# An encoder layer in split float32: two sums of a weight quad in one addition, and a fourth seven-product quad in four of eleven gate-and-up groups

## The chip, the cores and the metric

The kernel runs on one core of a Trainium2 chip. The metric is device time in microseconds (us) for one execution of the whole layer; the median of several executions is compared. Engines are named as in the profile: PE is the matrix engine (TensorE), DVE the vector engine, ACT the scalar engine, POOL is GpSimd and SP the engine whose queue issues most DMAs.

## The reference, cut to what matters

The layer takes x of 256 rows by 2048 columns, mixes tokens with two kinds of attention, and ends in a SwiGLU feed-forward block. Only that block is touched:

```python
D_MODEL = 2048; SEQ = 256; D_FF = 5632
gt, up = jnp.split(rms_norm(x, g_ffn) @ w_gate_up, 2, axis=-1)   # w_gate_up: 2048 x 11264
return x + (jax.nn.silu(gt) * up) @ w_down                       # w_down: 5632 x 2048
```

All arrays are float32.

## The kernel before

**Split products.** PE takes float32r operands here. Each float32 matrix is split into a high part (a cast to float32r, on ACT) and a low part (the value less its high part, on DVE); `split_pair` does this for weights. `mm3` then computes one product as three matmuls of 128 x 128 by 128 x 512: high by high, high by low, low by high (lines 427 to 429). A weight chunk costs one cast and one subtraction over its whole width before PE can use it.

**Parts, groups, quads.** The feed-forward block runs in five parts. Part one covers three blocks of 512 hidden columns, parts two to five cover two each. A part first computes one *gate-and-up group* per block (11 groups in all), then four *down groups*, which multiply the hidden block by `w_down` and add to the residual. A gate-and-up group walks 2048 input rows in eight *quads*, numbered 0 to 7. A quad holds two row blocks of 128 (kk = 0, 1) of the gate columns and of the up columns (n = 0, 1), so four weight blocks of 128 x 512, one chunk `x` in SBUF of shape 128 x 4 x 512. The 256 tokens are two halves (t = 0, 1). The group wants the four sums over kk of h[t, kk] times w[kk, n].

**Plain and fast quads.** A plain quad does this with eight products, 24 matmuls. A *fast* quad uses Winograd's scheme for two-by-two blocks: seven products, 21 matmuls, on sums of blocks. Before, quads 2, 4 and 6 of every group are fast (`FAST`). For a fast quad `split_fast` splits three of the raw weight blocks (`rh`, `rl`: the two blocks of kk = 1; `r`: the up block of kk = 0), then makes four sums in place in `x` with four additions of 512 columns (lines 844 to 847); `split` then splits the four sums (`wh`, `wl`). The token side has the same two forms, made once by `job_h`: `hP` for plain quads, `hs`, `hsh`, `hsl` (seven blocks) for fast ones.

**PSUM.** During the block the eight 512-column banks are held as tiles `mA`, `mB`, `sC`, `sD`. Fast-only products go to `mA` and `mB`, the rest to `sC` and `sD`, which plain quads use too. After a group's last fast quad `evac_fast` reads `mA` and `mB` (lines 663 to 667). After its last quad `evac_pair` reads `sC` and `sD` (lines 677 to 680), then come the silu (ACT, line 683) and the product with the up half (line 685). The next quad that writes `sC` waits for lines 678 and 679. The down groups use `mA`, `mB`, `sC` and again `mA`; line 703 adds them to the residual tiles `x1_0` to `x1_3`.

**Order and buffers.** The instructions of the block are recorded in program order, and a scheduler with priorities then sets the order on each engine; every engine runs its own list in order. Weight chunks have three buffers `x` (`xp`), and three pairs `wh`, `wl` (six buffers, `wp`). The load of chunk c therefore starts when the low part `wl` of chunk c - 3 is done, and the cast `wh` of chunk c can start when PE has finished chunk c - 3. Loads are DMAs of 512 KB, two to a chunk, issued by SP (line 826 for quads, line 835 for the rest). Everything else (`rh`, `rl`, `r`, `z`, `u`, `hs`, hidden tiles) shares 28 buffers of one size (`tp`).

**Chunk numbers.** In the listings of order below, `x253` is the chunk of quad 0 of part two's first group, `x254` that of quad 1, up to `x260` for quad 7; `x261` to `x268` are the part's second group, and `x250` to `x252` the last chunks of part one's down groups. The first group of part one has chunks 217 to 224.

Of the kernel before, what the change touches and what calls it, by code (L numbers as in the profile page):

```python
# [12 lines left out]
F32 = mybir.dt.float32  # L13
# [27 lines left out]
PRIO = 200  # L41
NPAIR = KD // 2
FAST = (2, 4, 6)


class Job:
    def __init__(self, gen, after=()):
        self.gen, self.after, self.ready, self.done = gen, tuple(after), 0, False
# [16 lines left out]


class Group:
    def __init__(self, w, c0, n, ks, lhs, evac, needs=None, sizes=None):
        self.w, self.c0, self.n, self.ks = w, c0, n, ks
        self.lhs, self.evac, self.needs = lhs, evac, needs or {}  # L70
        self.sizes = sizes


class Quad:


    def __init__(self, group, i):
        self.group, self.i, self.fast = group, i, i in FAST
        plain = [k for k in range(NPAIR) if k not in FAST]
        self.first, self.last = i == plain[0], i == plain[-1]  # L80
        self.first_fast, self.last_fast = i == FAST[0], i == FAST[-1]


class Flag:
# [11 lines left out]
def layer_kernel(ctx: ExitStack, tc: tile.TileContext, a: dict, out: bass.AP):  # L96
# [12 lines left out]
    def t4(shape, name, dt=F32):  # L109
        return tp.tile(shape, dt, name=name, tag="t4")  # L110
# [108 lines left out]
    def split_pair(h, l, x):  # L219
        nc.scalar.copy(h, x)  # L220
        nc.vector.tensor_sub(l, x, f32(h))  # L221

    class Act:


        def __init__(self, name, nk):
            self.name, self.nk = name, nk
            self.h, self.l = {}, {}
# [384 lines left out]
    def job_h(i):  # L613

        ps = half_side(f"tr_h{i}").rearrange("p (k s) -> p k s", s=S)
        for k in range(2):
            f = 2 * i + k
            for t in range(NT):
                nc.tensor.transpose(ps[:, k, t * P:(t + 1) * P], x1[f // 4][:, t, (f % 4) * P:(f % 4 + 1) * P], ident)
        g = [gain("g_ffn", 2 * i + k) for k in range(2)]  # L620
        if i not in FAST:
            hP[i] = t4([P, 2, 2, S], f"hP{i}", F32R)
            split_evac(*((hP[i][:, 0, k], hP[i][:, 1, k], ps[:, k], g[k]) for k in range(2)))
        else:
            v, l, h = t4([P, 8, P], f"hs{i}"), t4([P, 7, P], f"hsl{i}", F32R), t4([P, 7, P], f"hsh{i}", F32R)
            nc.scalar.activation(v[:, 0:8:7], ps[:, 0].rearrange("p (t s) -> p t s", t=NT), AF.Copy, scale=g[0])
            nc.scalar.activation(v[:, 1:3], ps[:, 1].rearrange("p (t s) -> p t s", t=NT), AF.Copy, scale=g[1])
            nc.vector.tensor_sub(v[:, 3], v[:, 7], v[:, 2])
            nc.vector.tensor_sub(v[:, 4], v[:, 7], v[:, 0])
            nc.vector.tensor_sub(v[:, 5], v[:, 0], v[:, 3])  # L630
            nc.vector.tensor_sub(v[:, 6], v[:, 1], v[:, 5])
            split_pair(h, l, v[:, :7])
            hq[i] = (h, l)
        return
        yield
# [34 lines left out]
    def evac_pair(half, i, last):  # L670

        def evac(zu, step):
            q = held["q"]
            z, u = zu
            add, sub = nc.vector.tensor_add, nc.vector.tensor_sub
            with tc.high_priority(offset=PRIO):
                add(z[:, 1], q[0], z[:, 1])
                add(z[:, 0], q[3], z[:, 0])
                add(u[:, 0], q[2], u[:, 0])  # L679
# [75 lines left out]
    for half, (j0, j1) in enumerate(PARTS):  # L755
        js = range(j0, j1)
        hidT[half] = Act(f"hid{half}", 4 * len(js))
        for i, j in enumerate(js):
            needs = {k: (lambda k=k: [hjobs[k]]) for k in range(NPAIR)}
            needs[FAST[0]] = lambda: list(hjobs.values())  # L760
            if i:
                needs[FAST[0]] = lambda half=half, i=i: [djobs[half, i - 1]]
            groups.append(Group(W["w_gate_up"], 512 * j, 1024, range(NPAIR), None, evac_pair(half, i, i == len(js) - 1), needs))
# [56 lines left out]
    def load(c):  # L820
        g, gi, ks, q = chunks[c]
        t = xt[c] = xp.tile([P, 4, 512], F32, name=f"x{c}", tag="x")
        if q:
            for kk in range(2):
                src = g.w[(2 * q.i + kk) * P:(2 * q.i + kk + 1) * P].rearrange("p (n f) -> p n f", n=2)
                nc.sync.dma_start(t[:, 2 * kk:2 * kk + 2], src[:, :, g.c0:g.c0 + 512])
            return
        if gi == 0 and c:
            load_x(ks[0] * P, (ks[-1] + 1) * P)
            if ks[-1] == KD - 1:  # L830
                load_rows()
        for o in range(0, len(ks), 2):
            sub = ks[o:o + 2]
            src = g.w[sub[0] * P:(sub[-1] + 1) * P, g.c0:g.c0 + g.n]
            nc.sync.dma_start(t[:, o:o + len(sub), :g.n], src.rearrange("(k p) n -> p k n", p=P))

    def split_fast(c):

        x = xt[c]
        rh, rl, r = (t4([P, 2, 512], f"{n}{c}", F32R) for n in ("rh", "rl", "r"))  # L840
        split_pair(rh, rl, x[:, 2:4])
        split_pair(r[:, 0], r[:, 1], x[:, 1])
        add = nc.vector.tensor_add
        add(x[:, 1], x[:, 0], x[:, 1])
        add(x[:, 0], x[:, 0], x[:, 2])
        add(x[:, 2], x[:, 1], x[:, 2])
        add(x[:, 3], x[:, 2], x[:, 3])  # L847
        raws[c] = {1: (r[:, 0], r[:, 1]), 3: (rh[:, 0], rl[:, 0]), 2: (rh[:, 1], rl[:, 1])}

    def split(c):  # L850
        g, gi, ks, q = chunks[c]
        if q and q.fast and c not in raws:
            split_fast(c)
        t = xt.pop(c)
        h = w8(f"wh{c}")
        h, l = (h, w8(f"wl{c}")) if gi >= ffn_at else (h[:, :2], h[:, 2:])
        s = (slice(None), slice(0, 4 if q else len(ks)), slice(0, 512 if q else g.n))
        split_pair(h[s], l[s], t[s])
        if q and q.fast:
            parts[c] = raws.pop(c) | {m: (h[:, n], l[:, n]) for n, m in enumerate((7, 5, 6, 4))}  # L860
        else:
            parts[c] = (h, l)

# [3 lines left out]
        return [j for k in ks if k in g.needs for j in g.needs[k]()]  # L867

    FACTOR = {1: 0, 2: 1, 4: 2, 5: 3, 7: 4, 6: 5, 3: 6}
    PLAIN = {(0, 0): 3, (0, 1): 2, (1, 0): 0, (1, 1): 4}  # L870

    def products_quad(c):
        q = chunks[c][3]
        bank, w = held["q"], parts.pop(c)
        if not q.fast:
            h, l = w
            for t, n in ((1, 0), (0, 0), (0, 1), (1, 1)):
                m = PLAIN[t, n]
                for kk in range(2):
                    s = slice(t * P, (t + 1) * P)  # L880
                    mm3(bank[m], hP[q.i][:, 0, kk, s], hP[q.i][:, 1, kk, s], h[:, 2 * kk + n], l[:, 2 * kk + n],
                        q.first and kk == 0, q.last and kk == 1)
# [177 lines left out]
```

## Time and profile before

| what | us |
|---|---|
| median of 3 runs | 1356.53 |
| lowest and highest of them | 1354.4 and 1360.9 |
| the profiled execution | 1356.11 |
| its span, first to last instruction | 1354.3 |
| PE busy within the span | 1339.5 |
| DVE busy | 949.1 |
| ACT busy | 652.2 |

The feed-forward block fills roughly the second half of the span, from about 635 us on. In the timeline a matmul row shows its start and a modelled duration of 0.39 us; matmuls overlap in the pipeline, so the distance between two starts is what one of them costs. The times of rows are us from the start of the span.

### The profile page before, as it was taken

To read this page: it belongs to the slowest core of one execution; us is meant where nothing else is said; L and a number is where in the kernel's file an instruction comes from. 1 tells how busy PE (TensorE), PEld (TensorE's weight loads), DVE (VectorE), ACT (ScalarE), POOL (GpSimd) and SP (SyncE) were. 2 spreads that over 40 slices of the span, in tenths; PEclk is the share of its full clock that TensorE was granted. 3 is DMA by queue.
4 is the path that set the end of the run, shared out by engine and by line. 5 is a ranking of instruction groups with operands and counts; after the bars stand their busy time and mean duration, and the time that the engine had idled before them with its cause. 6 is when DMAs were issued, how large, how long until landed. Compare 5 with 4: busy or idle time off the path is not lost.

```text
span 1354.3 us, 16169 instructions
## 1 busy us (share of the span) xinstructions
PE 1339.5 (99%) x6243; PEld 1126.0 (83%) x6243; DVE 949.1 (70%) x949; ACT 652.2 (48%) x724; POOL 34.3 (3%) x41
## 2 busy tenths in 40 slices
PE   8999999999999999999999999999999999999998
PEld 6899999988888888888788888888878888888886
DVE  5566777677645655567789756886798579857973
ACT  6455555454444444455455434454445345534541
POOL 1011112000000000000000000000000000000000
PEclk9999999999999999999999999999999999999999
DMA  7555555656556766676546665565457654754662
GB/s 247 179 175 161 161 170 167 184 161 176 174 186 205 212 188 202 209 235 207 201 158 213 221 187 183 191 213 190 157 185 245 191 186 172 229 190 163 214 214 93
DMA packets 138205, 257.14 MB, mean 190 GB/s; under 512 B 9192, under 2 KB 28688, under 8 KB 138128
## 3 DMA queue, kind: packets, MB, share of 16 engines
q1 hardware_dynamic: 137760, 255.96, 58.9%
q8 instruction: 49, 0.80, 0.2%
q14 instruction: 28, 0.23, 0.1%
q10 hardware_dynamic: 144, 0.13, 0.0%
q0 software_dynamic: 224, 0.01, 0.0%
HBM read 253.97 MB, written 2.10 MB: 189 GB/s over the span
## 4 chain that ended last, share of the span: by engine, by line
PE 94%; DVE 2%; issue 1%; DMA 1%; ACT 1%; SPq 0%; DVEq 0%; ACTq 0%
PE g L429 14%; PE g L427 14%; PE g L428 13%; PE sC L427 6%; PE sC L429 6%; PE sC L428 6%; PE mA L427 4%; PE mA L429 4%; PE mA L428 4%; PE sD L429 4%; PE sD L427 4%; PE sD L428 4%; PE mB L428 3%; PE mB L429 3%; PE mB L427 3%
## 5 line engine op out<-in xcount | busy, mean ns | idle before, releaser
L220 ACT CAST wh<-x 128x1024 fp32r<-128x1024 f32 (+3 forms) x349 | 465.3, 1352 | 437.0 <-DVE x L847 127.7
L221 DVE TENSOR_TENSOR wl<-x,wh 128x2048 fp32r<-128x2048 f32 x132 | 300.8, 2289 | 134.5 <-ACT wh L220 132.7
L221 DVE TENSOR_TENSOR wh<-x,wh 128x1024 fp32r<-128x1024 f32 (+2 forms) x217 | 250.6, 1172 | 113.1 <-ACT wh L220 111.9
L427 PE MATMUL g<-wh,xTh 128*128 128x512 f32 (+1 forms) x544 | 210.6, 387 | 0.6 <-ACT xTh L212 0.6
L429 PE MATMUL g<-wh,xTl 128*128 128x512 f32 (+1 forms) x544 | 207.9, 382 | 0.6 <-DVE xTl L217 0.6
L428 PE MATMUL g<-wh,xTh 128*128 128x512 f32 (+1 forms) x544 | 207.9, 382 | 0.0
L429 PEld LDWEIGHTS g<-wh,xTl 128*128 128x128 f32 x544 | 102.8, 189 | 17.6 <-DVE xTl L217 1.4
L427 PEld LDWEIGHTS g<-wh,xTh 128*128 128x128 f32 x544 | 102.8, 189 | 15.9 <-ACT xTh L212 0.9
L428 PEld LDWEIGHTS g<-wh,xTh 128*128 128x128 f32 x544 | 102.9, 189 | 15.4 <-DVE wh L221 0.4
L427 PE MATMUL sC<-wh,hP 128*128 128x512 f32 x220 | 86.1, 391 | 1.6 <-DVE u L679 1.5
L429 PE MATMUL sC<-wh,hP 128*128 128x512 f32 x220 | 85.7, 390 | 0.0
L429 PE MATMUL sD<-wh,hP 128*128 128x512 f32 x220 | 85.7, 389 | 0.0
L428 PE MATMUL sC<-wl,hP 128*128 128x512 f32 x220 | 85.7, 389 | 0.0
L427 PE MATMUL sD<-wh,hP 128*128 128x512 f32 x220 | 85.7, 389 | 0.0
L428 PE MATMUL sD<-wl,hP 128*128 128x512 f32 x220 | 85.7, 389 | 0.0
L220 ACT CAST rh<-x 128x1024 fp32r<-128x1024 f32 x33 | 34.7, 1051 | 36.1 <-DMA x<-in_w_gate_up_dram 36.1
L427 PEld LDWEIGHTS sC<-wh,hP 128*128 128x128 f32 x220 | 41.3, 188 | 12.3 <-issue 4.0
L427 PE MATMUL g<-wh,mTh 128*128 128x512 f32 x128 | 50.5, 394 | 0.0
L429 PE MATMUL g<-wh,mTl 128*128 128x512 f32 x128 | 49.9, 390 | 0.0
L428 PE MATMUL g<-wh,mTh 128*128 128x512 f32 x128 | 49.9, 390 | 0.0
L427 PEld LDWEIGHTS sD<-wh,hP 128*128 128x128 f32 x220 | 41.3, 188 | 8.6
L428 PEld LDWEIGHTS sD<-wl,hP 128*128 128x128 f32 x220 | 41.3, 188 | 8.6
(675 smaller groups left out, 2390.7 us busy)
## 6 DMA issues: line engine op xcount, KB each, us to landing
x<-in_w_gate_up_dram SPq DMA_DIRECT2D x176, 512.0 KB, 4.7
x<-in_w_down_dram SPq DMA_DIRECT2D x88, 512.0 KB, 5.0
x<-in_w_in_dram SPq DMA_DIRECT2D x79, 512.0 KB, 4.2
x<-in_w_in_dram SPq DMA_DIRECT2D x56, 448.0 KB, 3.6
x<-in_w_o_dram SPq DMA_DIRECT2D x32, 512.0 KB, 4.4
x<-in_w_o_mla_dram SPq DMA_DIRECT2D x16, 512.0 KB, 4.9
x<-in_w_o_dil_dram SPq DMA_DIRECT2D x16, 512.0 KB, 4.6
x<-in_w_ukv_dram SPq DMA_DIRECT2D x8, 512.0 KB, 4.0
```

The source lines that it names most:

```text
L220: nc.scalar.copy(h, x)
L221: nc.vector.tensor_sub(l, x, f32(h))
L427: nc.tensor.matmul(ps, ah, bh, start=first, stop=False)
L428: nc.tensor.matmul(ps, ah, bl, start=False, stop=False)
L429: nc.tensor.matmul(ps, al, bh, start=False, stop=last)
```

## The change

Three things change.

1. In `split_fast` the order of the two kk = 0 blocks in the chunk is swapped: up in place 0, gate in place 1. Two of the four sums (gate plus up of kk = 0, and gate of kk = 0 plus gate of kk = 1) then share the operand in place 1 and lie side by side, and one addition over 1024 columns, with that operand broadcast, makes both. Three additions remain in place of four, in every fast quad.
2. For that swap, a fast quad's kk = 0 blocks are loaded by two DMAs of 256 KB, one each, and the kk = 1 blocks by one of 512 KB as before: three DMAs in place of two.
3. In the first gate-and-up group of parts two to five quads 1, 3, 4 and 6 are fast (`FAST_1`), in all other groups 2, 4 and 6 as before. So there are 37 fast quads in place of 33. Token blocks 1 and 3 are needed in both forms now, so `job_h` makes the eight-block form (`EITHER`) for them, and splits eight blocks, not seven, for all of the five quads in `EITHER`; plain quads 1, 2 and 3 pick their factors from it by `BLOCK`.

```diff
 FAST = (2, 4, 6)
+FAST_1 = (1, 3, 4, 6)
+EITHER = tuple(sorted(set(FAST) | set(FAST_1)))
...
 def job_h(i):
-        if i not in FAST:
+        if i not in EITHER:
             hP[i] = t4([P, 2, 2, S], f"hP{i}", F32R)
...
-            v, l, h = t4([P, 8, P], f"hs{i}"), t4([P, 7, P], f"hsl{i}", F32R), t4([P, 7, P], f"hsh{i}", F32R)
+            v, l, h = (t4([P, 8, P], f"{n}{i}", d) for n, d in (("hs", F32), ("hsl", F32R), ("hsh", F32R)))
...
-            split_pair(h, l, v[:, :7])
+            split_pair(h, l, v)
...
-            needs[FAST[0]] = lambda: list(hjobs.values())
+            fast = FAST_1 if half and not i else FAST
+            needs[2] = lambda: list(hjobs.values())
             if i:
-                needs[FAST[0]] = lambda half=half, i=i: [djobs[half, i - 1]]
+                needs[2] = lambda half=half, i=i: [djobs[half, i - 1]]
...
 def load(c):
         if q:
             for kk in range(2):
+                if q.fast and kk == 0:
+                    for n in range(2):
+                        src = g.w[2 * q.i * P:(2 * q.i + 1) * P, n * DFF + g.c0:n * DFF + g.c0 + 512]
+                        nc.sync.dma_start(t[:, 1 - n], src)
+                    continue
                 src = g.w[(2 * q.i + kk) * P:(2 * q.i + kk + 1) * P].rearrange("p (n f) -> p n f", n=2)
                 nc.sync.dma_start(t[:, 2 * kk:2 * kk + 2], src[:, :, g.c0:g.c0 + 512])
...
 def split_fast(c):
         split_pair(rh, rl, x[:, 2:4])
-        split_pair(r[:, 0], r[:, 1], x[:, 1])
+        split_pair(r[:, 0], r[:, 1], x[:, 0])
         add = nc.vector.tensor_add
-        add(x[:, 1], x[:, 0], x[:, 1])
-        add(x[:, 0], x[:, 0], x[:, 2])
-        add(x[:, 2], x[:, 1], x[:, 2])
+        add(x[:, :2], x[:, 1:2].to_broadcast([P, 2, 512]), x[:, 0:3:2])
+        add(x[:, 2], x[:, 0], x[:, 2])
         add(x[:, 3], x[:, 2], x[:, 3])
...
+    BLOCK = {(0, 0): 0, (0, 1): 7, (1, 0): 1, (1, 1): 2}
 def products_quad(c):
+            def factors(kk, t):
+                if q.i in EITHER:
+                    return (z[:, BLOCK[kk, t]] for z in hq[q.i])
+                return (hP[q.i][:, e, kk, t * P:(t + 1) * P] for e in range(2))
```

**What moves on DVE.** This is DVE's list in the first group of part two, from the low part of quad 2's chunk (`wl255`) to that of quad 4's (`wl257`). Before:

```order
L221 TENSOR_TENSOR wl255_6410<-x255_6338,wh255_6409 128x2048
L221 TENSOR_TENSOR rl257_6441<-x257_6413,rh257_6440 128x1024
L221 TENSOR_TENSOR r257_6442<-x257_6413,r257_6442 128x512
L221 TENSOR_TENSOR wl256_6452<-x256_6381,wh256_6451 128x2048
L844 TENSOR_TENSOR x257_6413<-x257_6413 128x512
L845 TENSOR_TENSOR x257_6413<-x257_6413 128x512
L846 TENSOR_TENSOR x257_6413<-x257_6413 128x512
L847 TENSOR_TENSOR x257_6413<-x257_6413 128x512
L221 TENSOR_TENSOR wl257_6483<-x257_6413,wh257_6482 128x2048
```

After (its lines lie a few numbers further down; 852 is the wide addition, 853 and 854 the two others):

```order
L223 TENSOR_TENSOR wl255_6433<-x255_6361,wh255_6432 128x2048
L852 TENSOR_TENSOR x256_6393<-x256_6393 128x1024
L223 TENSOR_TENSOR rl257_6465<-x257_6436,rh257_6464 128x1024
L853 TENSOR_TENSOR x256_6393<-x256_6393 128x512
L223 TENSOR_TENSOR r257_6466<-x257_6436,r257_6466 128x512
L854 TENSOR_TENSOR x256_6393<-x256_6393 128x512
L852 TENSOR_TENSOR x257_6436<-x257_6436 128x1024
L853 TENSOR_TENSOR x257_6436<-x257_6436 128x512
L854 TENSOR_TENSOR x257_6436<-x257_6436 128x512
L223 TENSOR_TENSOR wl256_6475<-x256_6393,wh256_6474 128x2048
L223 TENSOR_TENSOR wl257_6503<-x257_6436,wh257_6502 128x2048
```

Quads 3 and 4 are both fast now, so the sums of two quads stand between `wl255` and `wl256`, where one plain split and the raw splits of one fast quad stood.

**The end of the same group on DVE.** After the change, from the low part of the next group's first chunk to the reads of `sC`:

```order
L223 TENSOR_TENSOR wl261_6632<-x261_6576,wh261_6631 128x2048
L666 TENSOR_TENSOR z1536_6660<-mA_5128,u1536_6661 128x512
L667 TENSOR_TENSOR u1536_6661<-mB_5129,z1536_6660 128x512
L668 TENSOR_TENSOR z1536_6660<-mB_5129,u1536_6661 128x512
L669 TENSOR_TENSOR z1536_6660<-mB_5129,z1536_6660 128x512
L223 TENSOR_TENSOR wl262_6678<-x262_6604,wh262_6677 128x2048
L680 TENSOR_TENSOR z1536_6660<-sC_5130,z1536_6660 128x512
L681 TENSOR_TENSOR u1536_6661<-sC_5130,u1536_6661 128x512
```

Nothing moved here: before, the same eight rows stand in the same order (lines 664 to 667, 678 and 679), the low part `wl262` ahead of the two reads of `sC`.

**SP's queue at the same place.** Before:

```order
L826 DMA x255_6338<-in_w_gate_up_dram 128x2x512 x2
L826 DMA x256_6381<-in_w_gate_up_dram 128x2x512 x2
L826 DMA x257_6413<-in_w_gate_up_dram 128x2x512 x2
L826 DMA x258_6455<-in_w_gate_up_dram 128x2x512 x2
L826 DMA x259_6486<-in_w_gate_up_dram 128x2x512 x2
```

After (line 831 is the 256 KB load, 834 the 512 KB load):

```order
L834 DMA x255_6361<-in_w_gate_up_dram 128x2x512 x2
L831 DMA x256_6393<-in_w_gate_up_dram 128x512 x2
L834 DMA x256_6393<-in_w_gate_up_dram 128x2x512
L831 DMA x257_6436<-in_w_gate_up_dram 128x512 x2
L834 DMA x257_6436<-in_w_gate_up_dram 128x2x512
L834 DMA x258_6478<-in_w_gate_up_dram 128x2x512 x2
L831 DMA x259_6506<-in_w_gate_up_dram 128x512 x2
L834 DMA x259_6506<-in_w_gate_up_dram 128x2x512
```

The kk = 1 blocks, which the first cast of a fast quad (`rh`) reads, now come as the third DMA of the chunk, behind two small ones.

More of the change, by code (lines that the diff above doesn't have):

```diff
@@ L67, with __init__ @@
 class Group:
-    def __init__(self, w, c0, n, ks, lhs, evac, needs=None, sizes=None):
+    def __init__(self, w, c0, n, ks, lhs, evac, needs=None, sizes=None, fast=FAST):
         self.w, self.c0, self.n, self.ks = w, c0, n, ks
         self.lhs, self.evac, self.needs = lhs, evac, needs or {}
-        self.sizes = sizes
+        self.sizes, self.fast = sizes, fast
 class Quad:
     def __init__(self, group, i):
-        self.group, self.i, self.fast = group, i, i in FAST
-        plain = [k for k in range(NPAIR) if k not in FAST]
+        self.group, self.i, self.fast = group, i, i in group.fast
+        plain = [k for k in range(NPAIR) if k not in group.fast]
         self.first, self.last = i == plain[0], i == plain[-1]
-        self.first_fast, self.last_fast = i == FAST[0], i == FAST[-1]
+        self.first_fast, self.last_fast = i == group.fast[0], i == group.fast[-1]
 class Flag:
@@ L759, in layer_kernel @@
             needs = {k: (lambda k=k: [hjobs[k]]) for k in range(NPAIR)}
-            needs[FAST[0]] = lambda: list(hjobs.values())
+            fast = FAST_1 if half and not i else FAST
+            needs[2] = lambda: list(hjobs.values())
             if i:
-                needs[FAST[0]] = lambda half=half, i=i: [djobs[half, i - 1]]
-            groups.append(Group(W["w_gate_up"], 512 * j, 1024, range(NPAIR), None, evac_pair(half, i, i == len(js) - 1), needs))
+                needs[2] = lambda half=half, i=i: [djobs[half, i - 1]]
+            groups.append(Group(W["w_gate_up"], 512 * j, 1024, range(NPAIR), None, evac_pair(half, i, i == len(js) - 1), needs, None, fast))
         for j in range(4):
@@ L859, in split @@
         if q and q.fast:
-            parts[c] = raws.pop(c) | {m: (h[:, n], l[:, n]) for n, m in enumerate((7, 5, 6, 4))}
+            parts[c] = raws.pop(c) | {m: (h[:, n], l[:, n]) for n, m in enumerate((5, 7, 6, 4))}
         else:
@@ L879, in products_quad @@
                 for kk in range(2):
-                    s = slice(t * P, (t + 1) * P)
-                    mm3(bank[m], hP[q.i][:, 0, kk, s], hP[q.i][:, 1, kk, s], h[:, 2 * kk + n], l[:, 2 * kk + n],
+                    mm3(bank[m], *factors(kk, t), h[:, 2 * kk + n], l[:, 2 * kk + n],
                         q.first and kk == 0, q.last and kk == 1)
```

## The prediction, written before the changed kernel ran

> **What bounds the kernel now.** I read the page's busy times first, then the stretches of the feed-forward block, then the chain of waits at the ends of groups, then the vector engine's instructions by form.
>
> ```profile
> span 1354.3 us, 16169 instructions
> PE 1339.5 (99%) x6243; PEld 1126.0 (83%) x6243; DVE 949.1 (70%) x949; ACT 652.2 (48%) x724; POOL 34.3 (3%) x41
> ```
>
> PE is busy 99% of the span. Ends of matmuls are modelled, so I take the price of a matmul from starts in the timeline: the first matmul of the first plain quad of part two, and the first of the next quad, 24 matmuls on.
>
> ```profile
> 830.51 0.39 PE L427 MATMUL sD<-wh,hP 128*128 128x512 f32 x1
> ...
> 835.96 0.39 PE L427 MATMUL sD<-wh,hP 128*128 128x512 f32 x1
> ```
>
> 5.45 us over 24 is 0.227 us each: a plain quad holds PE 5.45 us, a fast one 21 x 0.227 = 4.77. How near DVE is shows in the stretches (busy us by engine: PE, PEld, DVE, ACT, POOL): part one's down groups, then the first and the second gate-and-up group of part two.
>
> ```profile
> 770.00:831.00 61.00, 61.00 (x275) 50.64 (x274) 32.63 (x19) 23.22 (x14) 0.00 (x0) 1.00 0.60 190
> 831.00:873.00 42.00, 41.84 (x185) 34.40 (x184) 34.23 (x32) 20.27 (x16) 0.00 (x0) 1.00 0.60 202
> 873.00:920.00 47.00, 47.00 (x213) 38.83 (x212) 41.12 (x40) 23.95 (x19) 0.00 (x0) 1.00 0.59 199
> ```
>
> The granted clock is 1.00 in all three. DVE is busy 32.6 of 61 us in the down groups, 34.2 of 42 in the first group, 41.1 of 47 in the second. So PE bounds the block, and DVE is close behind in gate-and-up groups. The chain of waits (start, length) shows where DVE already decides, at the ends of the first groups of parts two and three:
>
> ```profile
> 870.89 0.68 DVE z L678
> 871.57 0.61 DVE u L679
> ...
> 872.31 0.47 PE sC L427
> ...
> 997.50 1.92 ACT wh L220
> ...
> 1001.65 0.61 DVE z L678
> 1002.27 0.68 DVE u L679
> ...
> 1003.08 0.47 PE sC L427
> ...
> 871.77 0.39 PE L429 MATMUL sD<-wh,hP 128*128 128x512 f32 x1
> ...
> 1001.80 0.39 PE L429 MATMUL sD<-wh,hP 128*128 128x512 f32 x1
> ```
>
> The next group's first matmul on `sC` starts 0.13 us after line 679 ends (871.57 + 0.61). Since the matmul before it PE has lost 872.31 - 871.77 - 0.23 = 0.31 us in part two, and 1003.08 - 1001.80 - 0.23 = 1.05 us in part three, where a cast `wh` came late ahead of lines 678 and 679.
>
> **The change, part by part.**
>
> *Fewer products.* Four quads lose one product of three matmuls: 12 x 0.227 = 2.7 us of PE time, on the path wherever nothing else ends last.
>
> *The wide addition.* The prices on DVE and ACT (mean ns behind the busy time, then idle time before and who ended it):
>
> ```profile
> L221 DVE TENSOR_TENSOR wl<-x,wh 128x2048 fp32r<-128x2048 f32 x132 | 300.8, 2289 | 134.5 <-ACT wh L220 132.7 <-PE g L429 1.0
> L221 DVE TENSOR_TENSOR rl<-x,rh 128x1024 fp32r<-128x1024 f32 x33 | 40.2, 1220 | 5.7 <-ACT rh L220 5.4
> L845 DVE TENSOR_TENSOR x<-x 128x512 f32<-128x512 f32 x33 | 22.8, 691 | 0.9
> L221 DVE TENSOR_TENSOR r<-x,r 128x512 fp32r<-128x512 f32 x33 | 22.6, 685 | 2.1 <-ACT r L220 2.1
> L220 ACT CAST wh<-x 128x2048 fp32r<-128x2048 f32 x132 | 250.2, 1910 | 310.4 <-DVE x L847 127.7 <-PE mA L428 58.1 <-PE mB L428 29.7
> L220 ACT CAST rh<-x 128x1024 fp32r<-128x1024 f32 x33 | 34.7, 1051 | 36.1 <-DMA x<-in_w_gate_up_dram 36.1
> L448 DVE TENSOR_TENSOR qk<-qk,mla0rr x1: 1225/1225/1225, 99.4 to 99.4; 128x1024 f32<-128x1024 f32 x1
> ```
>
> Line 448 is the nearest row: 1024 columns with a broadcast operand, in place, 1.23 us. Two additions of 0.69 are 1.38, so 0.15 us less per fast quad and one start between dependent additions less, 0.2 in all. In first groups and down groups it vanishes in DVE's waits for casts (132.7 us above). In second groups DVE has little idle time and PE reaches a low part just as it is done:
>
> ```profile
> 884.11 0.47 PE L427 MATMUL mB<-wh,hsh 128*128 128x512 f32 x1
> 884.43 0.39 PE L427 MATMUL sC<-rh,hsh 128*128 128x512 f32 x1
> ...
> 885.12 0.47 PE L428 MATMUL mB<-wl,hsh 128*128 128x512 f32 x1
> 885.43 0.39 PE L429 MATMUL mB<-wh,hsl 128*128 128x512 f32 x1
> ```
>
> Two steps of 0.32 and 0.31 where 0.227 is usual: about 0.2 us lost per group. Part one has two such groups, the others one each: six, so between 0 and -1.2; I take -0.3, since this may be the cost of any short wait.
>
> *One more quad of DVE work in four groups.* A fast quad costs DVE 1.22 + 0.69 + 1.23 + 2 x 0.69 = 4.5 us more than a plain one. Does it fit? I follow the first group of part two after the change, by these rows and its order. The load of a fast chunk takes, from the free buffer to the start of `rh`, 823.76 - (816.12 + 2.29) = 5.35 us (end of `wl` of chunk 252, then the cast of 255):
>
> ```profile
> 816.12 2.29 DVE L221 TENSOR_TENSOR wl<-x,wh 128x2048 fp32r<-128x2048 f32 x1 [3.15 <-ACT wh L220]
> 819.61 1.91 ACT L220 CAST wh<-x 128x2048 fp32r<-128x2048 f32 x1 [3.53 <-PE mA L428]
> 823.76 1.05 ACT L220 CAST rh<-x 128x1024 fp32r<-128x1024 f32 x1 [2.24 <-DMA x<-in_w_gate_up_dram]
> ```
>
> The cast of chunk 253 starts at 819.6, when PE frees its buffer; with `rl`, `r` and the wide addition of 254 ahead of it, `wl253` ends near 824.7. Then: load of 256 to 830.05, its `rh` to 831.1; DVE without a break `rl` 1.22, residual of line 703 1.22, `r` 0.69, `wl255` 2.29, the two quads' sums and the splits of 257 (2 x 1.22, 4 x 0.69, 1.22, 0.69), `wl256` 2.29, less 0.08 where independent ones follow each other: 845.3. Load of 259 to 850.7, `rh` to 851.7, `rl`, `r` and three sums to 856.3, cast to 858.2, `wl259` to 860.5. Load of 262 to 865.9, cast to 867.8. `wl262` cannot start before lines 666 to 669 end, near 868.05; it ends at 870.3, the reads of `sC` at 871.5, PE at 871.65. PE alone would be there at 872.0 - 0.68 = 871.3. So the wait stays near 0.3 us and the group gives its 0.68, with about 0.25 us to spare on this chain. Quad 3's low part is ready several us early, 4's (`wl256`, 845.3 against a use at 847.1) 1.8 us, 6's (860.5 against 862.0) 1.5 us. (The uses count PE's 5.45 and 4.77 per quad from 830.51, plus four matmuls.) A new wait is possible too: `mA` and `mB` are wanted by quad 1, one quad earlier, and line 703 now stands behind `rl256`; it ends at 833.5, quad 1 starts at 835.96, so 2.4 us of cover.
>
> *Part three* lost 1.05 us where part two lost 0.31, behind one late load there (a `rh` cast held 1.02 us):
>
> ```profile
> 966.86 1.06 ACT L220 CAST rh<-x 128x1024 fp32r<-128x1024 f32 x1 [1.02 <-DMA x<-in_w_gate_up_dram]
> ```
>
> If that does not come again it is -0.7; if it does, 0. I take -0.7.
>
> *Three DMAs for two.* Prices (KB each, median us to landing), and two issues on SP:
>
> ```profile
> x<-in_w_gate_up_dram SPq DMA_DIRECT2D x176, 512.0 KB, 4.7
> x<-in_w_in_dram SPq DMA_DIRECT2D x2, 256.0 KB, 3.5
> ...
> 2.63 0.47 SPq L835 DMA_DIRECT2D x<-in_w_in_dram  x1
> 860.41 1.20 SPq L826 DMA_DIRECT2D x<-in_w_gate_up_dram  x2
> ```
>
> 37 more issues of about 0.47 lie on SP, which waits for DVE between chunks. But the load that `rh` waits for is issued 0.94 us after the buffer is free, not 0.6. It may cost nothing, since it queues behind the same 512 KB as before; at most I allow the 1.0 us of the late load above. Two such loads (256, 259) lie on the chain with 0.25 to spare, so 0 to 1.8 us per first group; nearest is the difference in issue, 0.35 less what the queue hides, so +0.1 per group, +0.4.
>
> The Trainium skill, page "DMA: Bandwidth & Descriptors", section "Anatomy of one DMA — SWDGE (gpsimd) path", has a fixed cost of about 2.0 us per DMA plus bytes over 436 GB/s, and under "Bandwidth" it advises against small DMAs. By that fit, for another issuing path, 256 KB is an estimated 2.6 us and 512 KB 3.2, and in series a fast chunk would take 8.4 us instead of 6.4. The rows disagree: two loads of 4.7 are over 5.35 us after the first was issued, so fixed parts overlap.
>
> *The token side.* `job_h` for blocks 1 and 3 grows by a few small operations, in the output projection, where DVE has room; at the block's start PE's listed order puts four transposes two matmuls earlier. I take +0.1 (0 to 0.45). Two more of the 28 buffers are held; nothing in the part I followed waits for one: 0.
>
> Sum: -2.7 - 0.3 - 0.7 + 0.4 + 0.1 = -3.2 us on the profiled execution's 1356.1 (1354.3 of span and 1.8 around it). The median of the three runs is 0.4 higher, 1356.5; there it gives 1353.3.
>
> **The rivals.**
>
> *The group's end eats the gain.* Each first group loses at the reads of `sC` what part three already loses, 1.05 in place of 0.31. For it: 0.25 us to spare on a chain of three loads, 46 us long. Against: nothing on it is late by itself. Then parts two, four and five lose 0.74 each and part three gains nothing: 2.2 + 0.7 above the forecast, 1356.2.
>
> *Small loads come late everywhere: slower.* If the third DMA lands later by L in each fast quad, first groups lose 2L - 0.25 and the seven others, with three fast quads in DVE's busiest stretch, about L. At L = 1.0 that is 4 x 1.75 + 7 = 14 us in place of 0.4: 1367. It turns the case into slower by 0.5% from L near 0.75. Against: the casts `rh` have waited 36.1 us for loads already (their row above), and PE hardly felt it. The Trainium skill's fixed cost of that page, in series, would be this rival with L = 2, an estimate of 1382; I give it 0.01 of this rival's chance.
>
> *The wide addition costs more than two.* If sharing an operand that it overwrites took 2.5 us, DVE would gain 1.1 per fast quad; the seven groups with three would lose about 2.5 each and the four with four 3: 1383 at worst. Line 448 speaks against it.
>
> *All waits shrink: faster.* Second groups give the full 1.2, and DVE's saving closes the 0.3 at the ends of first groups and the wait of 649.54 - 648.30 - 0.23 = 1.0 at the block's start:
>
> ```profile
> 648.30 0.39 PE L428 MATMUL sC<-rl,hsh 128*128 128x512 f32 x1
> 649.54 0.66 PE L619 MATMUL mA<-ident,x 128*128 128x128 f32 x4 [0.85 <-ACT hs L627]
> ```
>
> That is -2.7 - 1.2 - 0.7 - 1.2 - 1.0 = -6.8: 1349.7, just at the bound.
>
> **How the numbers follow.** Forecast 0.62; gain eaten 0.24; late loads 0.06; dear addition 0.02; all waits shrink 0.06. Less than 0.5% (6.8 us) is about what a measurement of this kernel can't tell from no change; the first two cases and a third of the last lie inside: faster 0.04, same 0.88, slower 0.08 (late loads and the dear addition). The forecast's own range is 1351.3 (full 1.2 in second groups, loads for nothing, and 0.7 of scatter) to 1355.5; with the eaten gain and a scatter of runs of some 2 us (1354.4 to 1360.9 before) the range is 1350.0 to 1359.0.
>
> **What would show it.** In the profile after: 12 matmuls fewer; the wide addition at 1.22 to 1.23 us; the time from a free buffer to `rh` at 5.35 to 5.5 us; steps of PE at the first matmul on `sC` of second groups near 0.54 us in all four later parts, not 1.3; first groups shorter by 0.7. A step there of 1.3 or more means the second case, `rh` held everywhere the third, a mean of line 852 above 1.4 the fourth. The prediction is wrong if DVE's list in the fast pair 3 and 4 makes PE wait for `wl256` or `wl259`.

## The result, and the profile after

The changed kernel is slower: 1364.85 us median of 10 runs (1360.4 to 1369.6) against 1358.53 for the kernel before, a ratio of 1.0052 with a 95% interval of 1.0038 to 1.0067. The forecast was 1353.3 with a range up to 1359.0. The profiled execution took 1360.36 us, the shortest of the ten. Ratios here and below leave out three executions, one each of `e1_quads_only`, `e2_wide_split` and the kernel before, that took 9% or more longer than the rest. The page's head:

```profile
span 1358.4 us, 16286 instructions
PE 1336.6 (98%) x6231; PEld 1124.1 (83%) x6231; DVE 963.9 (71%) x942; ACT 662.4 (49%) x734; POOL 34.4 (3%) x41
```

The 12 matmuls are gone (6231), yet the span is 4.1 us longer. The same three stretches as in the prediction, shifted to the new start of the part (columns as there): down groups, first and second group of part two.

```profile
772.00:833.00 61.00, 61.00 (x275) 50.60 (x274) 33.75 (x20) 23.42 (x14) 0.00 (x0) 1.00 0.59 190
833.00:876.00 43.00, 41.21 (x182) 33.51 (x180) 36.20 (x32) 21.86 (x17) 0.00 (x0) 1.00 0.58 197
876.00:922.00 46.00, 46.00 (x207) 38.17 (x208) 40.47 (x38) 24.04 (x19) 0.00 (x0) 1.00 0.60 198
```

The first group is the one with gaps in PE, 41.21 of 43 us busy; DVE is still far from full (36.2). The larger gaps are at the first matmul on `sC` of the second groups (timeline, start and duration, in brackets the idle time and what ended it):

```profile
874.40 0.39 PE L431 MATMUL sD<-wh,hP 128*128 128x512 f32 x1
875.94 0.47 PE L429 MATMUL sC<-wh,hP 128*128 128x512 f32 x1 [1.15 <-DVE u L681]
...
1006.98 0.47 PE L429 MATMUL sC<-wh,hP 128*128 128x512 f32 x1 [2.13 <-DVE u L681]
...
1136.49 0.47 PE L429 MATMUL sC<-wh,hP 128*128 128x512 f32 x1 [1.13 <-DVE u L681]
...
1266.48 0.47 PE L429 MATMUL sC<-wh,hP 128*128 128x512 f32 x1 [2.05 <-ACT z L685]
```

The step in part two is 875.94 - 874.40 = 1.54 us, and in the others 2.5, 1.5 and 2.4; the forecast said 0.54. PE also waits inside the first groups, for the low part `wl259` of quad 6:

```profile
864.17 0.39 PE L429 MATMUL mA<-wh,hsh 128*128 128x512 f32 x1
865.20 0.50 PE L430 MATMUL mA<-wl,hsh 128*128 128x512 f32 x1 [0.64 <-DVE wl L223]
```

That is 865.20 - 864.17 - 0.23 = 0.80 us in part two, 0.54 and 0.40 at the same place in parts three and four, and nothing in part five. A wait for `wl259` is what the prediction named as a sign of being wrong. The chain of waits behind both (start, length) is one of loads:

```profile
849.84 5.26 DMA x<-in_w_gate_up_dram
...
855.12 1.06 ACT rh L222
...
860.91 1.92 ACT wh L222
...
862.85 2.30 DVE wl L223
...
865.17 0.54 SPq L834
...
865.75 4.51 DMA x<-in_w_gate_up_dram
...
870.36 1.92 ACT wh L222
...
875.12 0.69 DVE u L681
```

The first row is the third load of quad 6's chunk, 5.26 us by itself; `wl` at 862.85 is `wl259`. How long a fast chunk takes from the free buffer to `rh` is seen in the rows of chunks 251 to 256:

```profile
813.05 2.29 DVE L223 TENSOR_TENSOR wl<-x,wh 128x2048 fp32r<-128x2048 f32 x1 [3.15 <-ACT wh L222]
...
821.34 1.05 ACT L222 CAST rh<-x 128x1024 fp32r<-128x1024 f32 x1 [2.88 <-DMA x<-in_w_gate_up_dram]
...
822.81 1.91 ACT L222 CAST wh<-x 128x2048 fp32r<-128x2048 f32 x1
...
825.42 2.28 DVE L223 TENSOR_TENSOR wl<-x,wh 128x2048 fp32r<-128x2048 f32 x1
...
833.85 1.05 ACT L222 CAST rh<-x 128x1024 fp32r<-128x1024 f32 x1 [2.74 <-DMA x<-in_w_gate_up_dram]
```

821.34 - (813.05 + 2.29) = 6.00 and 833.85 - (825.42 + 2.28) = 6.15, where the kernel before had 5.35. In the whole kernel, by form, the wide addition costs what was forecast (1.221 us), and `rh` waits for its loads more than twice as long (78.0 us over 37, 36.1 over 33 before).

```profile
L852 DVE TENSOR_TENSOR x<-x 128x1024 f32<-128x1024 f32 x37 | 45.2, 1221 | 0.8
L222 ACT CAST rh<-x 128x1024 fp32r<-128x1024 f32 x37 | 38.9, 1052 | 78.0 <-DMA x<-in_w_gate_up_dram 77.9
...
x<-in_w_gate_up_dram SPq DMA_DIRECT2D x139, 512.0 KB, 5.0
x<-in_w_gate_up_dram SPq DMA_DIRECT2D x74, 256.0 KB, 2.9
```

The second place is the block's start, where the transposes of a last token block wait on PE for ACT's reads (`hs`) of the one before, 1.0 us before the change (timeline):

```profile
647.24 0.39 PE L431 MATMUL sC<-rh,hsl 128*128 128x512 f32 x1
650.30 0.66 PE L621 MATMUL mA<-ident,x 128*128 128x128 f32 x4 [2.68 <-ACT hs L629]
...
651.89 0.63 PE L430 MATMUL sD<-wl,hsh 128*128 128x512 f32 x1
652.31 0.63 PE L431 MATMUL sD<-wh,hsl 128*128 128x512 f32 x1
```

PE loses 650.30 - 647.24 - 0.23 = 2.8 us, and then matmuls start 0.42 us apart, not 0.227. The granted clock (the column before the last two, by stretch) is 0.64 there:

```profile
647.20:650.20 3.00, 0.43 (x2) 0.00 (x1) 0.99 (x2) 2.59 (x3) 0.00 (x0) 1.00 0.63 197
650.20:654.90 4.70, 4.60 (x16) 3.70 (x17) 3.50 (x6) 2.09 (x5) 0.00 (x0) 0.64 0.65 205
```

### The profile page after: what moved, and what is told of

It reads as the page before. It is cut to its first block, busy times and chain, and to the rows that moved or that the text cites. A ratio compares the mean times of both kernels' runs of the same rounds, so it can differ in the third digit from the quotient of the medians.

```text
span 1358.4 us, 16286 instructions
## 1 busy us (share of the span) xinstructions
PE 1336.6 (98%) x6231; PEld 1124.1 (83%) x6231; DVE 963.9 (71%) x942; ACT 662.4 (49%) x734; POOL 34.4 (3%) x41
## 4 chain that ended last, share of the span: by engine, by line
PE 79%; DVE 7%; DMA 7%; issue 3%; ACT 3%; SPq 1%; DVEq 0%; ACTq 0%
PE g L431 14%; PE g L429 14%; PE g L430 14%; DMA x<-in_w_gate_up_dram 6%; PE sC L429 3%; PE sC L431 3%; PE sC L430 3%; DVE wl L223 3%; PE sD L429 3%; PE sD L430 3%; PE sD L431 3%; PE mA L429 3%; PE mA L430 3%; PE mA L431 3%; PE mB L430 2%
## 5 line engine op out<-in xcount | busy, mean ns | idle before, releaser
L222 ACT CAST rh<-x 128x1024 fp32r<-128x1024 f32 x37 | 38.9, 1052 | 78.0 <-DMA x<-in_w_gate_up_dram 77.9
L223 DVE TENSOR_TENSOR rl<-x,rh 128x1024 fp32r<-128x1024 f32 x37 | 45.2, 1221 | 23.7 <-ACT rh L222 23.6
L429 PE MATMUL sC<-wh,hP 128*128 128x512 f32 x132 | 51.8, 393 | 6.7 <-DVE u L681 4.6
L431 PE MATMUL sC<-wh,hP 128*128 128x512 f32 x132 | 51.4, 389 | 0.0
L430 PE MATMUL sC<-wl,hP 128*128 128x512 f32 x132 | 51.4, 389 | 0.0
L430 PE MATMUL sD<-wl,hP 128*128 128x512 f32 x132 | 51.4, 389 | 0.0
L431 PE MATMUL sD<-wh,hP 128*128 128x512 f32 x132 | 51.4, 389 | 0.0
L429 PE MATMUL sD<-wh,hP 128*128 128x512 f32 x132 | 51.4, 389 | 0.0
L852 DVE TENSOR_TENSOR x<-x 128x1024 f32<-128x1024 f32 x37 | 45.2, 1221 | 0.8
L430 PE MATMUL sD<-wl,hsh 128*128 128x512 f32 x109 | 43.1, 396 | 0.0
```

The costliest lines, as they stand in the source:

```text
L429: nc.tensor.matmul(ps, ah, bh, start=first, stop=False)
L430: nc.tensor.matmul(ps, ah, bl, start=False, stop=False)
L431: nc.tensor.matmul(ps, al, bh, start=False, stop=last)
L852: add(x[:, :2], x[:, 1:2].to_broadcast([P, 2, 512]), x[:, 0:3:2])
```

## The experiments

All thirteen in one table. Ratios are to the kernel before, with 95% intervals. "Start" is the stretch from PE's first matmul on quad 0 to its fourth on quad 4 in part one's first group; "groups" is the sum of the first groups of parts two to five, each from its first matmul to the next group's. Both are worked out from one profiled execution. With the shortest group seen of each kind the four would take 4 x 41.80 = 167.2 us with three fast quads and 4 x 41.12 = 164.5 with four.

| kernel | loads | additions | fourth quad | ratio | start, us | groups, us |
|---|---|---|---|---|---|---|
| before, two profiles | 2 | 4 | no | 1 | 24.1, 24.0 | 167.9, 167.2 |
| changed, two profiles | 3 | 3 | yes | 1.0052 (1.0038 to 1.0067) | 27.2, 28.8 | 172.5, 174.6 |
| `e1_quads_only` | 2 | 4 | yes | 1.0024 (1.0009 to 1.0039) | 26.2 | 171.1 |
| `e2_wide_split` | 3 | 3 | no | 0.9994 (0.9982 to 1.0006) | 26.9 | 168.6 |
| `e3_wide_two_loads` | 2 | 3 | yes | 0.9980 (0.9964 to 0.9995) | 26.1 | 165.3 |
| `e4_split_only` | 3 | 4 | no | 1.0027 (1.0015 to 1.0038) | 29.4 | 169.0 |
| `e5_wide_two_loads_fast` | 2 | 3 | no | 0.9965 (0.9953 to 0.9978) | 23.7 | 167.7 |
| `e6_kk1_first` | 2, swapped | 3 | yes | 1.0000 (0.9989 to 1.0010) | 26.7 | 170.7 |
| `e9_big_load_first` | 3, swapped | 3 | yes | 1.0205 (1.0190 to 1.0221) | 27.2 | 182.4 |
| `e10_token_side_only` | 2 | 4 | no, but its token blocks | 1.0029 (1.0016 to 1.0042) | 29.7 | 168.4 |
| `e11_1246` | 2 | 3 | yes, quads 1, 2, 4, 6 | 0.9991 (0.9979 to 1.0003) | 27.4 | 165.8 |
| `e15_late_tokens` | 2 | 3 | yes, token blocks later | 0.9963 (0.9951 to 0.9975) | 25.1 | 165.3 |
| `e16_late_tokens_three_loads` | 3 | 3 | yes, token blocks later | 1.0047 (1.0030 to 1.0064) | 27.5 | 174.8 |

The two profiled executions of the kernel before took 1356.1 and 1355.1 us, below its medians of 1358 to 1359, so a typical run of it takes some 3 us more than they show.

**The four quads alone.** The changed kernel without the load loop of line 831, with the four additions of before.

> The four quads alone: the first groups of parts two to five have the four fast quads 1, 3, 4 and 6, but the four additions of 512 columns and the two loads of 512 KB per fast chunk stay as in the kernel before. Theory A (three loads make the first cast of a fast chunk late; the fourth quad itself fits): a fast chunk lands 5.35 us after its first issue as before, the step of PE at the first matmul on sC of the four second groups stays near 0.55 us (at most 0.8, since DVE has 0.2 us more to do per quad), no wait for wl259, and each first group is 0.5 to 0.7 us shorter: time 0.997 to 0.999 of before, span near 1351.5. Theory B (the pair of fast quads 3 and 4 with the fourth quad's work on DVE is what makes the group's end late): the steps there are 1.3 us or more as in the changed kernel, and the time is 1.000 to 1.003 of before.

Measured 1.0024: neither theory. In parts four and five, where no load came late, the group lost nothing and gained nothing (41.93 and 41.79 us against 41.80): the 0.68 us of PE's work came back as a step at `sC` of 1.36 and 1.21 us. Parts two and three lost more (42.60 and 44.77); there a fast chunk on the chain landed 6.0 and 6.9 us after its first issue, in parts four and five 5.3 to 5.5. So with four additions the fourth quad does not fit, even with two loads.

**The wide addition with three loads, no fourth quad.** `FAST` everywhere, seven-block `job_h`.

> The wide addition and the three loads without the fourth quad: every group has the fast quads 2, 4 and 6. Theory A (the loads): the third load lands 5.9 us after the first issue, not 5.35, on a chain of two fast chunks per first group; less the slack, the steps of PE at sC in the second groups grow from 0.55 to 0.8 to 1.5 us, and the block's start loses 2 to 3.5 us as in the changed kernel (a wait of 2.8 us and eight matmuls at 0.43 us): time 1.002 to 1.005 of before. Theory B (the fourth quad): everything as before, 0.999 to 1.001.

Measured 0.9994, as theory B said. Theory A failed in three groups of four: parts two, three and four took 41.80 us, the chain with three fast quads hides the later load. Part five took 43.24, with a step of 1.99 at `sC` as theory A has it, and theory A held at the block's start (26.9). Against the wide addition with two loads (below) the three loads still cost 0.0029, so the 0.9994 is a gain and a loss together.

**All of the change with two loads.** The gate and up blocks of a fast quad go to every other place, so that one DMA fills two of them:

```diff
-                nc.sync.dma_start(t[:, 2 * kk:2 * kk + 2], src[:, :, g.c0:g.c0 + 512])
+                at = t[:, 1 - kk::2] if q.fast else t[:, 2 * kk:2 * kk + 2]
+                nc.sync.dma_start(at, src[:, :, g.c0:g.c0 + 512])
...
-        add(x[:, :2], x[:, 1:2].to_broadcast([P, 2, 512]), x[:, 0:3:2])
-        add(x[:, 2], x[:, 0], x[:, 2])
-        add(x[:, 3], x[:, 2], x[:, 3])
+        add(x[:, :2], x[:, 1:2].to_broadcast([P, 2, 512]), x[:, 0:4:3])
+        add(x[:, 3], x[:, 0], x[:, 3])
+        add(x[:, 2], x[:, 3], x[:, 2])
```

> The changed kernel with two loads of 512 KB per fast chunk again: the gate and up blocks of kk = 0 go to places 1 and 3 by one load, those of kk = 1 to places 0 and 2 by the other, so that the wide addition still has its operands in order. Everything else of the change stays. Theory A (the loads): a fast chunk lands 5.35 us after its first issue, the steps at sC are near 0.55 us, the first groups are 0.7 us shorter each, the block's start loses at most 0.5 us: time 0.996 to 0.999 of before. Theory B (the fourth quad): steps of 1.3 us or more stay, 1.001 to 1.004.

Measured 0.9980, 0.0072 below the changed kernel: theory A, in size too in the groups. In part five the second group starts 0.55 us after the matmul before it:

```profile
1258.12 0.39 PE L431 MATMUL sD<-wh,hP 128*128 128x512 f32 x1
1258.67 0.47 PE L429 MATMUL sC<-wh,hP 128*128 128x512 f32 x1 [0.16 <-DVE u L681]
```

Parts four and five take 41.12 us, 0.68 less than before, parts two and three 41.35 and 41.72. The block's start still lost 2 us, which theory A had not expected.

**The three loads alone.** The kernel before with the kk = 0 blocks of fast quads in two DMAs.

> The three loads alone: the kernel before, with the two blocks of kk = 0 of a fast quad loaded by two DMAs of 256 KB into the same places as before. Four additions, fast quads 2, 4 and 6 everywhere. Theory A (the loads): steps at sC of 0.8 to 1.5 us, first cast of a fast chunk 0.55 to 0.75 us later, the block's start 0.5 to 3 us longer: time 1.002 to 1.005 of before. Theory B (the fourth quad) and theory C (the wide addition's place in the order): 0.999 to 1.001.

Measured 1.0027, as theory A said, but mostly not in the groups it named: 169.0 us, 1 to 2 more than before, and 29.4 at the block's start.

**The wide addition alone,** with two loads.

> The wide addition with two loads of 512 KB and without the fourth quad (quads 2, 4 and 6 in every group): what the wide addition alone is worth. Theory A' (the wide addition pays only where a group's chain of loads has no slack): first groups 41.80 us as before, second groups 0.1 us shorter as in the runs with the wide addition, so -0.5 to -1.5 us: 0.9985 to 1.000 of before, and within 0.001 of the same kernel with three loads (0.9994). Rival (three loads cost in every group): 0.002 less than with three loads, about 0.997.

Measured 0.9965, the rival: 0.0029 less than with three loads. This is the smallest edit that beats both kernels.

**The order of a fast quad's loads.** Two loads with kk = 1 first, and the changed kernel's three with the 512 KB of kk = 1 first: `for kk in (1, 0) if q.fast else (0, 1):`.

> The four quads and the wide addition with two loads of 512 KB, and for fast quads the kk = 1 blocks, which the first cast reads, are loaded first. Theory A' (the chain of loads decides the first groups): rh starts 4.1 us after the first issue instead of 5.4; with the order of loads of before, the first groups already gave their 0.68 us and PE itself ended them, so no more than 0.5 us in all is left there; at the block's start the chain of two fast chunks is 1 to 2 us shorter: 0.996 to 0.998 of before. Rival (the order of loads doesn't matter, since the sums need the other load too): 0.998 as with the two loads in the old order.

> The changed kernel with the three loads of a fast chunk in another order: the 512 KB of kk = 1 first, then the two of 256 KB. Theory A' (what is late in the changed kernel is the load that rh waits for, since it stands third): rh starts near 4.1 us after the first issue, the first groups give 0.4 to 0.7 us each instead of losing 0.8 to 1.25, time 0.996 to 0.999 of before. Rival (it is the number of loads: the chunk is complete only when the third has landed, 5.9 us after the first issue, and the sums wait for it): steps of PE at sC of 1 us or more stay, 1.001 to 1.004.

Both missed, the second by 2%. `rh` does start earlier in both, 4.4 and 4.3 us at the median after the buffer is free. But the scheduler, which sets each engine's order, now puts the raw splits of the next group's fast quad ahead of the reads of `sC`. DVE at the end of part two's first group in the first of the two:

```profile
870.76 0.69 DVE L667 TENSOR_TENSOR u<-mB,z 128x512 f32<-128x512 f32 x1
872.05 1.23 DVE L223 TENSOR_TENSOR rl<-x,rh 128x1024 fp32r<-128x1024 f32 x1 [0.59 <-ACT rh L222]
873.19 0.68 DVE L668 TENSOR_TENSOR z<-mB,u 128x512 f32<-128x512 f32 x1
873.79 0.68 DVE L669 TENSOR_TENSOR z<-mB,z 128x512 f32<-128x512 f32 x1
874.39 0.68 DVE L223 TENSOR_TENSOR r<-x,r 128x512 fp32r<-128x512 f32 x1
874.99 1.22 DVE L848 TENSOR_TENSOR x<-x 128x1024 f32<-128x1024 f32 x1
876.12 0.68 DVE L680 TENSOR_TENSOR z<-sC,z 128x512 f32<-128x512 f32 x1
```

Between the two reads of `mB` DVE waits for the cast `rh`, which waited for its load, then does `rl`, `r` and the wide addition of chunk 263 before `sC` is read. These two runs tell what an order costs, not what the load's position costs.

**The kernel before, once more.**

> The kernel before, unchanged, for a second profile. Question: the wait of PE at the block's start, 1.0 us in the first profile of before, is 2.5 to 3.8 us in the changed kernel and in four versions of it, with two loads or three. Theory S (scatter: the six loads of the first three chunks crowd between 615 and 629 us, and how much differs by execution): 2 us or more here too. Theory O (the order of PE, ACT or DVE in the changed versions makes it): 1.0 us again.

The wait was 0.9 us again, so theory S fails as it stands.

**The token side alone.** `EITHER = (1, 2, 3, 4, 6)` with `FAST` in every group.

> The token side alone: blocks 1 and 3 get the eight-block form in job_h and plain quads take their factors from it, but no group has a fourth fast quad, and additions and loads are those of before. Theory T (the heavier token blocks make the first loads of the block late): the stretch from quad 0 to quad 4 of part one's first group is 1.8 to 2.3 us longer, as in the two versions with four quads and two loads, and PE waits 3 us or more for hs there in place of 1.2; the groups are as before: 1.001 to 1.002 of before. Rival (it costs what the prediction said, 0.1 us): 1.000.

Measured 1.0029, even more than theory T said: 29.7 us at the block's start, 5.6 more than before. PE waits 4.0 us for `hs` where it waited 0.85, and then runs at half its clock until 659.9:

```profile
654.04 1.11 PE L621 MATMUL mA<-ident,x 128*128 128x128 f32 x4 [4.03 <-ACT hs L629]
```

**Quads 1, 2, 4 and 6**: `FAST_1` so, with two loads and the wide addition.

> The wide addition with two loads and four fast quads in the first groups of parts two to five, but quads 1, 2, 4 and 6 in place of 1, 3, 4 and 6, so that only one more token block (1) has the eight-block form. Theory T: the block's start loses half, 0 to 1.2 us, and the first groups give their 0.68 us if the pair of fast quads 1 and 2, which starts with DVE idle from the down groups, leaves the chain of loads in time: 0.994 to 0.997 of before, below the wide addition alone (0.9965). Rival (four quads have no room in any place, or the block's start loses as much): 0.997 to 0.999.

Measured 0.9991. The groups give nearly all (165.8), but one more eight-block token block costs the block's start as much as two.

**The changed kernel, once more.**

> The changed kernel, unchanged, for a second profile. Theory: the same waits in the same places, 2.5 us or more at the block's start and 1.3 to 2.5 us at sC in the four second groups, since they come from the order and the loads; what differs is the granted clock after them. Rival (they are scatter of one execution): other places and sizes.

1368.3 us, with a span of 1366.4: the same places, some of the sizes larger than expected. The steps at `sC` are 1.83, 3.37, 1.69 and 1.72 us, the wait at the block's start 4.5. The waits for quad 6's low part are 1.6 us in part two and 1.4 in part four.

**The token blocks made later.** Plain forms of blocks 1 and 3 as before; in part one's down groups their halves are added up again and the eight-block form is made:

```diff
+    def late_h(i):
+        p, (v, l, h) = hP.pop(i), heavy(i)
+        for k, s in ((0, slice(0, 8, 7)), (1, slice(1, 3))):
+            hi, lo = (f32(p[:, e, k]).rearrange("p (t s) -> p t s", t=NT) for e in range(2))
+            nc.vector.tensor_add(v[:, s], hi, lo)
+        sums(i, v, l, h)
...
+    for i in (1, 3):
+        at(gidx("evac_down"), lambda i=i: late_h(i), -6 * i)
```

> The wide addition with two loads and the four quads 1, 3, 4 and 6, but the eight-block forms of token blocks 1 and 3 are made in part one's down groups, from the sum of the high and low parts of their plain forms, and not in the output projection; block 2 is still split in eight blocks there. Theory T (these blocks in the output projection make the first loads of the block come bunched and late): the block's start is as in the kernel before (16.2 and 7.6 us for the two stretches from quad 0 to quad 4), the down groups hide the new work, the first groups give 0.45 to 0.8 us each: 0.993 to 0.996 of before, 2 us below the wide addition alone. Rival (the block's start loses because of something else in these versions): 0.997 to 0.999 as with the blocks in the output projection.

> The changed kernel, three loads and all, but with the eight-block forms of token blocks 1 and 3 made in part one's down groups. What is left against the version with two loads is what the three loads cost in the presence of the four quads. Theory A' (three loads: 1.5 to 2 us per first group and 2 to 3 us at the block's start): 0.0065 to 0.009 more than with two loads, about 1.001 to 1.004 of before. Rival (the token side was nearly all of the loss): 0.996 to 0.999.

Measured 0.9963 and 1.0047. With two loads the start falls to 25.1, not to 24, and the total lies between the two expectations, level with the wide addition alone. With three loads nearly all of the loss stays (0.0084 more than with two), the difference that theory A' gave, with a total just above its 1.004: most of the changed kernel's loss is the loads'.

## Why the prediction was wrong

**The step that failed: three DMAs for two.** The prediction allowed 0 to 1.8 us per first group for the later load and took +0.1, "nearest is the difference in issue, 0.35 less what the queue hides". Nothing was hidden. The third load is issued 849.84 - 848.99 = 0.85 us after the buffer is free and takes 5.26 us; before, the second is issued after 0.58 us and took 4.8 at the median. From free buffer to `rh` it is 6.0 to 6.15 us, not 5.35, and two or three such loads stand in series in a chain with 0.25 us to spare. So the prediction's own sign came, PE's wait for `wl259`, but from the loads and not from DVE's list: with two loads PE waits for it in no part. Against the same kernel with two loads, part by part, the first groups lose 1.70, 2.05, 1.50 and 1.89 us, 7.1 in all. The ratios of four pairs of kernels differ by 0.0027 and 0.0029 for the third load with three fast quads, 0.0072 and 0.0084 (9.8 and 11.4 us) with four. How the chain of part two ran, in us from the group's first matmul:

| | forecast | changed | with two loads |
|---|---|---|---|
| low part `wl253` done | -5.8 | -5.2 | -6.0 |
| `rh256` starts | -0.5 | 1.0 | -0.6 |
| low part `wl256` done | 14.8 | 16.1 | 13.8 |
| `rh259` starts | 20.2 | 22.2 | 20.6 |
| low part `wl259` done (PE could use it at 31.5) | 30.0 | 32.3 | 30.4 |
| cast of chunk 262 starts | 35.4 | 37.5 | 35.8 |
| next group's first matmul | 41.1 | 43.1 | 41.4 |

Row 1 is a second, smaller slip: I followed DVE's list and not ACT's. There the cast of chunk 253 stands behind `rh` and `r` of chunk 254 (822.81 behind 821.34 in the rows above), so it waits for that load too and started 0.8 us after PE had freed its buffer (819.6 in the forecast, 2.4 us later here, as the whole part is). Between rows 2 and 3 the two kernels differ by the order as well: with two loads the scheduler puts `wl256` ahead of the last sum of chunk 257, 0.69 us.

**This was the second of the rivals,** "small loads come late everywhere". Its price for first groups, 2L - 0.25, gives 1.35 at L = 0.8; measured are 1.25, 1.24, 0.83 and 1.21 on top of before (the part-three value counts from 42.53); the second profile scatters more, 2.31, 1.72, 2.06 and 0.53. I gave it 0.06 because `rh` had waited 36.1 us for loads "and PE hardly felt it": those were quads with slack. Its other half was wrong: second groups lost nothing (42.50 us against 42.61), save one of 43.97 in the second profile, where the clock was halved.

**The token side** was put at +0.1, at most 0.45. Alone it measures 1.0029, 3.9 us (2.2 to 5.7), nearly all at the block's start (5.6 us in the profiled execution, 0.5 in the groups). There the wait for `hs` moves with one event, the landing of the first fast chunk (219): in all five profiles with four additions the transposes start 23.0 us after its `rh`, here in the kernel before (649.54, in the prediction), and with the token side alone (654.04); with the wide addition it is 21.3 to 22.7 us.

```profile
626.56 1.05 ACT L220 CAST rh<-x 128x1024 fp32r<-128x1024 f32 x1 [2.08 <-DMA x<-in_w_gate_up_dram]
```

```profile
631.05 1.05 ACT L222 CAST rh<-x 128x1024 fp32r<-128x1024 f32 x1 [3.62 <-DMA x<-in_w_gate_up_dram]
```

In the kernel before the first three chunks are issued 2.7 us apart and the last of the six loads lands 6.5 us after its chunk's first issue; in all versions with heavier token blocks or three loads they come 1.4 to 2.6 us apart, and it lands 7.6 to 8.8 us after. That the heavier blocks alone cost this much the timed runs show; that they do it by delaying the splits that free the buffers is read from that one profile, where the block's first load is issued at 618.40 and not at 614.56. Why three loads alone do the same is not shown: up to that point their lists on DVE and ACT are those of before, and their splits part from before's at 597 us, 23 us ahead of the first changed load. One profile of each cannot tell that from chance.

**The granted clock** was not in the prediction as a cost. Its mean over ten runs is 0.9969, over 34 of the kernel before 0.9987: about 2.5 of the 6.4 us between the mean spans (1363.2 and 1356.8). It falls after long waits of PE (last section), so a wait that the change adds can cost a second time.

**What held.** Twelve matmuls fewer, part three's stall as one late load (the second profile of before has 41.80 us there), the wide addition at 1.22 us, 0.68 us per first group where the loads come in time. The wide addition itself was put at -0.3 (0 to -1.2) and measures -4.8 us (-6.4 to -3.0): 0.1 us per second group is seen, 0.3 at the block's start, and 1.4 in the granted clock (0.9996 against 0.9986); the rest lies in waits that the profiled executions of before don't show, and stays open.

## What to carry to other kernels

In a chain of load, split, free buffer, load, a DMA more per link can cost at every link, here 0.65 to 0.8 us, even if the bytes are the same; first look for a layout that one strided DMA can fill. When you forecast such a chain, follow the list of every engine on it, and price each long wait that it adds also by the granted clock. And after an edit that only reorders loads, read the new order of the compute engines before believing in an earlier load.

## What the runs showed of the hardware

**Half clock after a wait.** After PE waited, the granted clock went to half for 3.4 us (6.8 in a few places), and matmuls started 0.427 us apart (eight in the changed kernel, 1.6 us lost). It is not a matter of length alone. With the four quads alone PE waited 3.1 us at the block's start and kept its clock, and 2.1 us at `sC` in part three and lost it:

```profile
651.10:655.10 4.00, 4.00 (x20) 3.39 (x21) 2.79 (x6) 1.46 (x3) 0.00 (x0) 1.00 0.34 96
...
1007.30:1011.30 4.00, 4.00 (x11) 3.15 (x12) 4.00 (x7) 1.23 (x2) 0.00 (x0) 0.57 0.83 262
```

The Trainium skill, page "TensorE: Matmul & The Clock Gate", section "Part 1: The HAM clock gate (the "warmup" mystery)", has half rate after an idle window of about 3.4 us that runs freely, and 426.7 ns per matmul of 512 columns when cold. The spacing and the length of the slow stretch agree; that a wait of 2.1 us sufficed is shorter than the window that the Trainium skill gives there.

What decides can be read from the clock that the traces record. In every trace the half-clock stretches between the first 30 and the last 10 us last 3.41 or 6.83 us, and they start whole multiples of 3.413 us apart: 654.33 and 1012.73 in the second profile of the changed kernel, 105 of them. I cut the 15 traces into such windows and summed PE's idle time in each. Each of the 18 windows with 2.06 us or more was followed by half clock; none of the 21 with 1.2 to 1.9 us was. The wait of 3.1 us above is split by a window's edge at 649.18 into 1.2 and 1.9 us, and the one of 2.1 us lies in one window.

**Loads in a row overlap in part.** 256 KB land 2.9 us after issue, near the estimate of 2.6 us that the prediction drew from the Trainium skill, page "DMA: Bandwidth & Descriptors", section "Anatomy of one DMA — SWDGE (gpsimd) path". In series the three would by that estimate take 8.4 us. Measured from the first issue to the last landing, the fast chunks issued after the chunk ahead had landed took 5.9 us (median of 13), and chunks of two loads in the kernel before 5.4 (median of 42).
